# Hybrid decoder trunk on one core: another order of hooks and projection steps in the retention layer

## The chip, the core and the metric

The kernel runs on one core of one Trainium2 chip. TensorE multiplies matrices, VectorE (DVE), ScalarE (ACT) and GpSimd (POOL) work on elements, and SyncE (SP) issues DMAs. The metric is the device time of one execution in microseconds, lower is better.

## The reference

The trunk has two layers on 512 tokens of width 1024, in float32. The first mixes tokens by a gated MLP, the second by retention with 4 heads (key width 256, value width 512, chunks of 128); each is followed by a dense MLP of width 4096 with squared ReLU. The change lies in the second layer's mixer:

```python
def retention(xn, w_in, head_norm_g, w_out):
    proj = xn @ w_in                                   # (512, 1024) @ (1024, 6144)
    q, k, v, g = jnp.split(proj, [H * dk, 2 * H * dk, 2 * H * dk + H * dv], axis=-1)
    q, k = rotary(q, cos, sin), rotary(k * dk ** -0.5, cos, sin)
    ...
    # per chunk and head: o = (q k^T * decay) v + (q * decay) state ; state = state * decay + (k * decay)^T v
    ...
    o = rmsnorm(o, head_norm_g)
    o = o * jax.nn.silu(g)
    return o @ w_out

x = x + retention(rmsnorm(x, norm_mix_g[1]), ...)
x = x + squared_relu_mlp(rmsnorm(x, norm_ffn_g[1]), ...)
```

## The kernel before

**Precision.** Every float32 product is made of three TensorE passes over high and low parts (`mm3`, L290). Each weight tile `raw` is split into `wH` by a cast on ACT (L243) and `wL` by a subtraction on DVE (L250); both must be there before the matmuls of the tile.

**Fewer products.** The large projections (v, g and the output) are done as seven products of half blocks instead of eight (`seven`). Some products need sums of weight blocks: a base is loaded by SP (L173), and a second block is added to it in place by an accumulating DMA that GpSimd issues (L216). Some need sums of activations ("side sums": DVE L610 to L630, with a cast on ACT, L627). A product's result lands in a PSUM bank and is added by DVE into `vF` or `gF` (L512).

**Stages of the retention layer.** q and k are projected in `qk` steps of 24 matmuls (the script's `Q` and `q`, two for q and two for k of each head); v of heads 0 and 1 in steps `v`, of heads 2 and 3 in `w`; the gates g in `g` and `j`; the output in `o`. These have 12 matmuls each, only the last `o` has 24. The first `Q` has 48. The layer has no loop over chunks: all causal score blocks of a head are computed at once (`sc`, key chunk j against queries from j on), multiplied by the decay on DVE into `pm` and split (pH by ACT, pL by DVE), and multiplied with v (`av`, query chunk n, n+1 blocks of 3 matmuls). Then DVE multiplies with the gate into `gF` (L1194), ACT squares and sums (`sqh`, L1195), DVE and GpSimd form the norm's factor (`msh`, L1197; `rh`, L337) and ACT rescales `gF` (L1199). `yt` transposes a head's output on TensorE and ACT writes it to `ryF` (L1213).

**What sets the order.** The whole layer is one script, a string that `play` reads word by word. Each word runs the next step of the letter's stream: `v`, `g` and so on; after the step's matmuls are issued and the next weight tiles are prepared (three steps ahead), the actions in its brackets run, the hooks. Every engine takes its instructions in the order in which the program issues them, so the script fixes the order on all of them. `+G`, `+w` and `+j` make a stream's first weights known to the loader. I number steps by letter from 1: v11 is the eleventh `v`. The words of the hooks that matter here:

- `f3`: side sums 3 for the v projection; `k3`: store these sums to DRAM (L1056, SP); `F3`: fetch them back for the `w` projection into the tile `spx` (L1062, GpSimd), or form them anew for 0, 2 and 6. A step that needs a sum that isn't there calls for it itself.
- `R`: the token norm's factors; `p0`, `p1`: from here the rope (L1127 to L1137, DVE and ACT) of head 0's q and k may run.
- `sc01`: scores of head 0, key chunk 1; `av013`: outputs of head 0 for query chunks 1 and 3; `yt0013`: transposes of head 0, columns 0, 1, 3. `vs01`: the value split of chunk 1 (L1110 ACT, L1111 DVE); `si01`: silu of the gate (L1118).
- `T`: put the residual tokens away to DRAM; `t0`: bring half of them back (L1233). `y0`: fetch head 0's transposed output (L1222).
- `o10`: side sum 1 of the output projection, half 0. `X` and `x`: lend a further buffer (`more`) to the weight loads, and take it back.

`sc`, `av` and the first two `yt` of a head share two small PSUM banks.

Of the kernel before, what the change touches and what calls it, by code (L numbers as in the profile page):

```python
# [18 lines left out]
T = 512  # L19
# [69 lines left out]
def trunk(ctx, tc, x, norm_mix_g, norm_ffn_g, a_w_in, a_b_in, a_v_norm_g, a_w_s, a_b_s, a_w_out,  # L89
# [729 lines left out]
    def play(script, act, early, **streams):  # L819

        left = {k: list(v) for k, v in streams.items()}
        for word in script.split():
            if word[0] == "+":
                r = early[word[1]]
                assert r[0] not in raws
                raws.extend(r)
                continue
            name, _, rest = word.partition("(")
            todo = [act(w) for w in rest.rstrip(")").split(",") if w]
            hook = (lambda todo=todo: [(advance(), f()) for f in todo]) if todo else None  # L830
            if name == "-":
                do(hook)
            else:
                left[name].pop(0)(hook)
        assert not any(left.values()), left
# [418 lines left out]
    def act(word):  # L1254
# [22 lines left out]
    qs = [r for h in range(H) for r in qk_steps(h)]  # L1277
    do(begin_values)
    play("""
        Q(w0,f1) v v(R) v(k1) v(p0) v v(f3) q q(f5,f4) v v(k5) v(p1) v v v v +G v(T,sc00) g g g g(sc03,k4) g(vs0320) g  # L1280
        q(sc01) g g(k3) q(si00) g(sc02) g(F1) q g(si021,av00) g(vs01) q g q(si03,si110,sc10,av023) g(F4,av01,sc13) +w
        w(F3,sc12,yt02,si132,sc11) q(vs10123,yt0013,X) q(av101) w(x,av123) q(yt11) w(yt1320,sc20) w(sc21) w(sc22) w w
        w q(sc23) w(F5) w +j w w w j(X) w j q j j j j j j(vs2120) q(si210,t0,av20) j(vs23) j q j(si232,av221) j(y0)
        j(y1,o00,si31,av23) j(sc30,sc32,sc31,t1,o01,vs30) o(yt21,sc33) o o(vs3123,si302,o50,yt20)
        o(av301,o51,si33,av32,yt223) o(av33) o(o10) o(yt30123) o o o o(o20,o31) o o o o(o30) o o(o40,o21,o11) o o(o41)
        o o o(o60) o o o(o61) o o
    """, act, {"G": tG[:1], "w": tV[1:], "j": tG[1:], "o": tO}, v=prodV[0], g=prodG[0], w=prodV[1], j=prodG[1], o=prodO,
        Q=qs[:1], q=qs[1:])
    may["extra"] = True
# [143 lines left out]
```

## Time and profile before

| | |
|---|---|
| runs | 1633.93, 1333.93, 1336.11 us; median 1336.11 |
| the profiled execution | 1335.48 us, its span 1333.8 |
| mean granted TensorE clock | 0.993 |
| busy: PE, DVE, ACT, POOL | 98%, 65%, 53%, 11% of the span |
| retention layer | about 605 to 993 us of the span |

The profile is of one execution. Times within it count from the span's start. A row of the timeline gives start, length, engine, source line, operation, the tiles written and read, and in brackets how long the engine was idle before and what ended that. Matmul rows overlap their neighbours: the pace is the distance between starts.

### The profile page before, as it was taken

What the parts mean: (1) busy time and instruction counts of PE and PEld (TensorE: products, weight loads), DVE (VectorE), ACT (ScalarE), POOL (GpSimd) and SP (SyncE); (2) the same over time, 40 slices, a digit from 0 to 9 for tenths busy, and PEclk for the clock granted to TensorE, in tenths of its full rate; (3) what the DMA queues carried; (4) which work ended last, traced back from release to release, by engine and by line L of the source; (5) the groups of instructions that cost most, each with busy time, mean ns of one, the idle gap of its engine ahead of it and who ended that gap; (6) DMA issues with size and microseconds to landing.
All of it is one profiled execution on the core that took longest, in us unless ns stands there. A gap on an engine that the chain in (4) does not pass through costs nothing.

```text
span 1333.8 us, 15231 instructions
## 1 busy us (share of the span) xinstructions
PE 1307.0 (98%) x5914; PEld 1083.9 (81%) x5914; DVE 863.4 (65%) x1089; ACT 701.0 (53%) x1033; POOL 149.5 (11%) x130
## 2 busy tenths in 40 slices
PE   9999999999999999999999998998999999999997
PEld 7888887888888888888787886886888888888885
DVE  5654489844656655888855664566973565655697
ACT  5555544654445444655544662556754445444554
POOL 1000242000100001001100120012100000100003
PEclk9999999999999999999999999998999999999999
DMA  9765468751765759685997486779746475676763
GB/s 323 190 166 183 86 187 221 192 157 65 160 187 152 196 158 207 167 211 161 270 255 243 134 254 197 168 244 249 170 115 189 96 195 175 149 207 157 191 173 95
DMA packets 143065, 243.25 MB, mean 182 GB/s; under 512 B 4161, under 2 KB 56977, under 8 KB 140945
## 3 DMA queue, kind: packets, MB, share of 16 engines
q1 hardware_dynamic: 106192, 166.24, 36.4%
q0 software_dynamic: 36480, 75.50, 31.4%
q8 instruction: 46, 0.75, 0.2%
q10 hardware_dynamic: 320, 0.53, 0.1%
q14 instruction: 27, 0.21, 0.0%
HBM read 231.78 MB, written 10.49 MB: 182 GB/s over the span
## 4 chain that ended last, share of the span: by engine, by line
PE 88%; DVE 5%; DMA 2%; ACT 2%; issue 2%; POOL 1%; ACTq 0%; POOLq 0%; DVEq 0%
PE up L290 24%; PE u L290 6%; PE qk L290 5%; PE smwa L290 3%; DVE wL L250 2%; PE v L878 2%; PE smwc L290 2%; PE smroa L290 2%; PE smyoa L290 2%; PE v L290 2%; PE sm12a L290 2%; PE sm11a L290 2%; PE sm10a L290 2%; PE sm02a L290 2%; PE sm01a L290 2%
## 5 line engine op out<-in xcount | busy, mean ns | idle before, releaser
L250 DVE TENSOR_TENSOR wL<-raw,wH 128x1024 fp32r<-128x1024 f32 x263 | 326.5, 1250 | 157.9 <-issue 58.3
L243 ACT CAST wH<-raw 128x1024 fp32r<-128x1024 f32 x263 | 272.8, 1046 | 116.7 <-DMA raw<-in_b_w_in_dram 27.9
L290 PE MATMUL up<-hH,wH 128*128 128x512 f32 x480 | 186.7, 389 | 0.0
L290 PE MATMUL up<-hL,wH 128*128 128x512 f32 x480 | 186.7, 389 | 0.0
L290 PE MATMUL up<-hH,wL 128*128 128x512 f32 x480 | 186.7, 389 | 0.0
L978 ACT ACTIVATE aF<-up 128x512 f32<-128x512 f32 x60 | 36.0, 599 | 219.1 <-PE up L290 219.1
L250 DVE TENSOR_TENSOR wL<-more,wH 128x1024 fp32r<-128x1024 f32 x64 | 79.0, 1236 | 60.1 <-issue 34.1
L290 PEld LDWEIGHTS up<-hL,wH 128*128 128x128 f32 x480 | 90.1, 188 | 18.8
L290 PEld LDWEIGHTS up<-hH,wH 128*128 128x128 f32 x480 | 90.1, 188 | 18.7
L290 PEld LDWEIGHTS up<-hH,wL 128*128 128x128 f32 x480 | 90.1, 188 | 18.6
L216 POOL DMA_DIRECT2D raw<-in_mlp_w_dram x27 | 35.8, 1406 | 507.2 <-DMA raw<-in_mlp_w_dram 209.2
L243 ACT CAST wH<-more 128x1024 fp32r<-128x1024 f32 x64 | 66.9, 1047 | 30.3 <-PE sm11a L290 3.4
L630 DVE TENSOR_TENSOR sp<-aF,sp 128x512 fp32r<-128x512 f32 x48 | 31.0, 687 | 52.1 <-ACT sp L627 52.1
L290 PE MATMUL u<-hH,wH 128*128 128x512 f32 x128 | 50.2, 392 | 0.0
L290 PE MATMUL u<-hL,wH 128*128 128x512 f32 x128 | 49.8, 389 | 0.0
L290 PE MATMUL u<-hH,wL 128*128 128x512 f32 x128 | 49.8, 389 | 0.0
L290 PE MATMUL qk<-hH,wH 128*128 128x512 f32 x112 | 44.5, 397 | 1.3 <-DVE gF L512 1.3
L290 PE MATMUL qk<-hH,wL 128*128 128x512 f32 x112 | 44.3, 396 | 0.9 <-DVE wL L250 0.9
L290 PE MATMUL qk<-hL,wH 128*128 128x512 f32 x112 | 44.2, 395 | 0.0
L979 ACT ACTIVATE aF<-aF 128x512 f32<-128x512 f32 x64 | 40.5, 633 | 2.0
L742 ACT ACTIVATE gu<-uz,gT 128x512 f32<-128x512 f32 x16 | 11.6, 724 | 51.3 <-DVE uz L741 51.3
L216 POOL DMA_DIRECT2D raw<-in_b_w_in_dram x16 | 21.2, 1361 | 146.8 <-DVE wL L250 72.1
(512 smaller groups left out, 2943.7 us busy)
## 6 DMA issues: line engine op xcount, KB each, us to landing
raw<-in_mlp_w_dram SPq DMA_DIRECT2D x48, 1024.0 KB, 5.6
raw<-in_mlp_w_dram POOLq DMA_DIRECT2D x27, 1024.0 KB, 8.3
raw<-in_b_w_in_dram SPq DMA_DIRECT2D x26, 1024.0 KB, 7.3
more<-in_mlp_w_dram SPq DMA_DIRECT2D x24, 1024.0 KB, 5.3
raw<-in_b_w_in_dram POOLq DMA_DIRECT2D x16, 1024.0 KB, 9.7
raw<-in_a_w_in_dram SPq DMA_DIRECT2D x8, 1024.0 KB, 5.9
raw<-in_b_w_out_dram POOLq DMA_DIRECT2D x8, 1024.0 KB, 9.4
morew<-in_a_w_in_dram SPq DMA_DIRECT2D x7, 1024.0 KB, 7.9
```

The source lines that it names most:

```text
L216: nc.gpsimd.dma_start(out=r.tile, in_=src, accum_op=ALU.add)
L243: nc.scalar.copy(out=p.hi, in_=p.src)
L250: nc.vector.tensor_sub(out=p.lo, in0=p.src, in1=f32(p.hi))
L290: nc.tensor.matmul(ps, lhsT=a, rhs=b, start=start and i == 0, stop=stop and i == 2, skip_group_check=resumed)
L630: nc.vector.tensor_sub(out=lo, in0=vs[c], in1=f32(hi))
L742: nc.scalar.activation(gu[j][:, c, :], z, AF.Gelu_apprx_tanh, bias=gT[:, BU + f : BU + f + 1])
L878: nc.tensor.matmul(accs0[n], lhsT=h[kk][:, n * P : (n + 1) * P], rhs=w, start=kk == 0 and j == 0, stop=kk == 7 and j == 2)
L978: nc.scalar.activation(a, ps, AF.Relu)
L979: nc.scalar.activation(a, a, AF.Square)
```

## The change

Only the script of the retention layer is rewritten. No instruction is added or taken away: TensorE has 5250 rows of order and VectorE 989 in either kernel. What moves is the step at whose hook an action stands, the place of some `q` and `j` steps among the others, and with these the order of weight loads and accumulations.

```diff
@@ -1277,13 +1277,13 @@
     qs = [r for h in range(H) for r in qk_steps(h)]
     do(begin_values)
     play("""
-        Q(w0,f1) v v(R) v(k1) v(p0) v v(f3) q q(f5,f4) v v(k5) v(p1) v v v v +G v(T,sc00) g g g g(sc03,k4) g(vs0320) g
-        q(sc01) g g(k3) q(si00) g(sc02) g(F1) q g(si021,av00) g(vs01) q g q(si03,si110,sc10,av023) g(F4,av01,sc13) +w
-        w(F3,sc12,yt02,si132,sc11) q(vs10123,yt0013,X) q(av101) w(x,av123) q(yt11) w(yt1320,sc20) w(sc21) w(sc22) w w
-        w q(sc23) w(F5) w +j w w w j(X) w j q j j j j j j(vs2120) q(si210,t0,av20) j(vs23) j q j(si232,av221) j(y0)
-        j(y1,o00,si31,av23) j(sc30,sc32,sc31,t1,o01,vs30) o(yt21,sc33) o o(vs3123,si302,o50,yt20)
-        o(av301,o51,si33,av32,yt223) o(av33) o(o10) o(yt30123) o o o o(o20,o31) o o o o(o30) o o(o40,o21,o11) o o(o41)
-        o o o(o60) o o o(o61) o o
+        Q(w0,f1,k1) v(R) v v v(p0) v v q(f3) q(f5,f4) v v(p1) v v v(k5) v v(sc00) v +G g(T) g g g(sc03) g(k4,vs0320)
+        g(sc01) q g g(sc02) q(si01) g(k3,si00) g(vs01,F1) q q(av00) g(si03) g(av013,si02) g(av02) g(si110,sc10)
+        q(vs10123,sc11,F4) +w w(sc13,sc12,si132,F3) q(yt0013,X,yt02) q(av10123) w q w(yt10) w(yt12) w(x,yt113,sc20)
+        w(F5) q(X,sc21,sc23) w w w w(sc22) +j w w j w j w q j j j j j j j(vs20) q j(y0,vs23,si20,vs212,av20) q(si2132)
+        j(av212) j j(y1,o00,si31,t0,av23) j(sc30,sc33,sc32,sc31,t1,vs30) o(vs3123) o(si302,o50,yt20) o(yt21)
+        o(av32,o51,yt223,si33,av301) o(av33,o10) o o(yt30123) o o(o20,o01) o o(o31) o o o(o30) o(o60) o(o21)
+        o(o40,o11) o o(o41) o o o o(o61) o o o o
     """, act, {"G": tG[:1], "w": tV[1:], "j": tG[1:], "o": tO}, v=prodV[0], g=prodG[0], w=prodV[1], j=prodG[1], o=prodO,
         Q=qs[:1], q=qs[1:])
     may["extra"] = True
```

In the old script's terms: `k1`, `f3`, `k5`, `T`, `k4` and `k3` move by one to three steps, `p1` from v9 to v8; q6 stands ahead of g11 and g12 and carries `av00`; `av` of head 0 is spread over q6, g12 and g13, that of head 1 put together in the hook of q9; `F5` moves from w9 to w6 and q11 from behind w8 to behind w6; j1 and j2 stand ahead of w13 and w14; `t0` moves from q13 to j13; head 3's score block 3 moves from o1 to j14, and in o4 `av32` stands ahead of `av30` and `av31`; `o10`, `o20`, `o30`, `o60` and `o61` move to earlier o steps.

Three places show this in the engines' order. The first is VectorE around the rope of head 0's k, at v8 to v11 (`qkL_4632` and `qkL_4634` are its low parts, `smvc` a bank of the v projection). Before:

```order
L250 TENSOR_TENSOR wL_4867<-raw_4713,wH_4866 128x1024
L250 TENSOR_TENSOR wL_4883<-raw_4765,wH_4882 128x1024
L1127 TENSOR_TENSOR m_4908<-qk_4778,wide 128x512
L1128 TENSOR_TENSOR m_4911<-qk_4778,wide 128x512
L1129 TENSOR_TENSOR m_4909<-qk_4807,wide 128x512
L1130 TENSOR_TENSOR m_4910<-qk_4807,wide 128x512
L1131 TENSOR_TENSOR m_4908<-m_4908,m_4909 128x512
L1132 TENSOR_TENSOR m_4910<-m_4910,m_4911 128x512
L1137 TENSOR_TENSOR qkL_4632<-m_4908,qkH_4631 128x512
L1137 TENSOR_TENSOR qkL_4632<-m_4910,qkH_4631 128x512
L250 TENSOR_TENSOR wL_4905<-raw_4765,wH_4904 128x1024
L512 TENSOR_TENSOR vF_4775<-vF_4775,smvc_4727 128x512
```

and now:

```order
L250 TENSOR_TENSOR wL_4867<-raw_4713,wH_4866 128x1024
L1127 TENSOR_TENSOR m_4888<-qk_4771,wide 128x512
L1128 TENSOR_TENSOR m_4891<-qk_4771,wide 128x512
L1129 TENSOR_TENSOR m_4889<-qk_4807,wide 128x512
L1130 TENSOR_TENSOR m_4890<-qk_4807,wide 128x512
L1131 TENSOR_TENSOR m_4888<-m_4888,m_4889 128x512
L1132 TENSOR_TENSOR m_4890<-m_4890,m_4891 128x512
L1137 TENSOR_TENSOR qkL_4634<-m_4888,qkH_4633 128x512
L1137 TENSOR_TENSOR qkL_4634<-m_4890,qkH_4633 128x512
L250 TENSOR_TENSOR wL_4883<-raw_4765,wH_4882 128x1024
L250 TENSOR_TENSOR wL_4917<-raw_4765,wH_4916 128x1024
L512 TENSOR_TENSOR vF_4768<-vF_4768,smvc_4727 128x512
```

Of the two weight splits ahead of the rope's eight instructions, the second (`wL_4883`) is now behind them.

The second place is GpSimd from q5 to w9: `raw` tiles are accumulations of weights, `spx` are the fetched sums (the first of each list are sums 1, the last sums 5), `rh` the norm factors of one query chunk each. Before:

```order
L1062 DMA spx_5334<-sums_4694 128x2048
L216 DMA raw_5369<-in_b_w_in_dram 128x4x512
L337 TENSOR_TENSOR rh<-msh,mhalf 128x1 x3
L1062 DMA spx_5581<-sums_5113 128x2048
L337 TENSOR_TENSOR rh<-msh,mhalf 128x1
L1062 DMA spx_5627<-sums_5236 128x2048
L216 DMA raw_5369<-in_b_w_in_dram 128x4x512
L337 TENSOR_TENSOR rh<-msh,mhalf 128x1 x4
L216 DMA raw_5877<-in_b_w_in_dram 128x4x512
L216 DMA raw_5880<-in_b_w_in_dram 128x4x512
L216 DMA raw_5369<-in_b_w_in_dram 128x4x512
L1062 DMA spx_6108<-sums_4888 128x2048
```

and now:

```order
L216 DMA raw_5337<-in_b_w_in_dram 128x4x512
L1062 DMA spx_5342<-sums_4631 128x2048
L337 TENSOR_TENSOR rh<-msh,mhalf 128x1 x4
L1062 DMA spx_5617<-sums_5133 128x2048
L1062 DMA spx_5663<-sums_5316 128x2048
L216 DMA raw_5337<-in_b_w_in_dram 128x4x512
L337 TENSOR_TENSOR rh<-msh,mhalf 128x1 x4
L216 DMA raw_5877<-in_b_w_in_dram 128x4x512
L216 DMA raw_5880<-in_b_w_in_dram 128x4x512
L1062 DMA spx_6007<-sums_4956 128x2048
L216 DMA raw_5337<-in_b_w_in_dram 128x4x512
```

The accumulation that stood behind the first fetch stands ahead of it, no fetch stands between head 0's four `rh`, and the fetch of sums 5 stands ahead of the third accumulation into the same tile (`raw_5369` before, `raw_5337` now), behind the two that precede it.

The third place is ScalarE at o4 and o5, around the outputs of head 3 (`av_6877` before and `av_6845` now are its query chunk 2). Before:

```order
L1213 ACTIVATE ryF_6754<-yt_6821,gT 128x512
L243 CAST wH_6839<-raw_6679 128x1024
L1195 ACTIVATE sqh_6850,ssh<-av_6845 128x512
L1199 ACTIVATE gF_6378<-gF_6378,rh 128x512
L1195 ACTIVATE sqh_6863,ssh<-av_6855 128x512
L1199 ACTIVATE gF_6378<-gF_6378,rh 128x512
L627 CAST spro_6868<-saro_6869 128x512 x2
L1118 ACTIVATE gF_6378<-gF_6378,r_80 128x512
L1195 ACTIVATE sqh_6888,ssh<-av_6877 128x512
```

and now:

```order
L1213 ACTIVATE ryF_6798<-yt_6821,gT 128x512
L243 CAST wH_6839<-more_6042 128x1024
L1195 ACTIVATE sqh_6856,ssh<-av_6845 128x512
L1199 ACTIVATE gF_6378<-gF_6378,rh 128x512
L627 CAST spro_6861<-saro_6862 128x512 x2
L1213 ACTIVATE ryF_6798<-yt_6869,gT 128x512
L1213 ACTIVATE ryF_6798<-yt_6875,gT 128x512
L1118 ACTIVATE gF_6378<-gF_6378,r_80 128x512
L1195 ACTIVATE sqh_6887,ssh<-av_6882 128x512
```

The first square behind the cast was that of query chunk 0, and is that of chunk 2 now; the chunks 0 and 1 follow behind the two transposes of head 2. The cast ahead reads `raw_6679` before, and the lent tile `more_6042` now.

## The prediction

> **What bounds the kernel now.** I read the page's busy times first, then the windows over the retention layer (605 to 993 us of the span), then the waits of TensorE there, and then the rows around each wait.
>
> ```profile
> span 1333.8 us, 15231 instructions
> PE 1307.0 (98%) x5914; PEld 1083.9 (81%) x5914; DVE 863.4 (65%) x1089; ACT 701.0 (53%) x1033; POOL 149.5 (11%) x130
> 605.00:992.00 387.00, 372.47 (x1675) 307.42 (x1673) 264.39 (x358) 212.74 (x321) 49.86 (x45) 0.98 0.78 211
> 720.00:740.00 20.00, 17.80 (x71) 13.96 (x70) 11.26 (x15) 8.19 (x11) 1.88 (x2) 0.91 0.56 140
> 800.00:820.00 20.00, 15.00 (x63) 12.29 (x62) 6.68 (x8) 4.40 (x5) 0.00 (x0) 0.91 0.81 224
> 890.00:935.00 45.00, 39.28 (x176) 31.59 (x175) 29.36 (x46) 28.63 (x50) 8.82 (x8) 0.92 0.85 223
> 935.00:1000.00 65.00, 64.64 (x307) 53.74 (x306) 56.39 (x72) 42.49 (x66) 5.16 (x4) 1.00 0.61 144
> ```
>
> The columns of a window are its length, then the busy time and count of PE, PEld, DVE, ACT and POOL, the granted clock, the DMA share and GB/s. The kernel is bound by TensorE: 1307.0 of 1333.8 us. In the retention layer PE is idle 387.00 - 372.47 = 14.5 us, and three windows hold nearly all of it (2.2 + 5.0 + 5.7), with the clock at 0.91 or 0.92 in the same three. That bounds the change: no matmul is added or removed, so it can save the stalls and slow stretches and no more, some 20 us, while 2% of this kernel is 26.7 us.
>
> ```profile
> PE smwa L290 <- DMA spx<-sums: 5.0, 1, 5.0
> PE av L290 <- ACT sqh L1195: 4.0, 1, 4.0
> ```
>
> These are the two longest of PE's waits there (the columns: total, times, longest). Each occurs once, as do the shorter ones, so the change is priced place by place, in program order. What a wait costs beyond itself is seen at the stall in the first of the three windows:
>
> ```profile
> 728.68 0.39 PE L290 MATMUL smga<-wH,hL 128*128 128x512 f32 x1
> 730.33 0.47 PE L290 MATMUL qk<-hH,wH 128*128 128x512 f32 x1 [1.26 <-DVE gF L512]
> 730.64 0.39 PE L290 MATMUL qk<-hL,wH 128*128 128x512 f32 x1
> 731.97 0.61 PE L290 MATMUL qk<-hH,wL 128*128 128x512 f32 x1 [0.94 <-DVE wL L250]
> 735.36 0.52 PE L290 MATMUL qk<-hL,wH 128*128 128x512 f32 x1
> 735.72 0.40 PE L290 MATMUL qk<-hH,wL 128*128 128x512 f32 x1
> ```
>
> Matmuls start 0.23 us apart at the full clock, but from 731.97 to 735.36 eight steps take 3.39 us, 0.42 each: about 1.6 us lost after the waits have ended. The whole stall: 730.33 - 728.68 - 0.23 = 1.4, 731.97 - 730.64 - 0.23 = 1.1, and the 1.6, in sum 4.1. I call the last part the gate's price, 1.7 with its edges.
>
> **Place 1, v10 to v13 (k, f3, p1 moved).** `p1` now comes one v step earlier, so the rope of head 0's k stands ahead of a weight split on DVE which stood ahead of it.
>
> ```profile
> 647.84 3.49 DVE L250 TENSOR_TENSOR wL<-raw,wH 128x1024 fp32r<-128x1024 f32 x3
> 651.24 0.68 DVE L1127 TENSOR_TENSOR m<-qk,wide 128x512 f32<-128x512 f32 x1
> 655.00 1.29 DVE L1137 TENSOR_TENSOR qkL<-m,qkH 128x512 fp32r<-128x512 f32 x2
> 656.21 1.22 DVE L250 TENSOR_TENSOR wL<-raw,wH 128x1024 fp32r<-128x1024 f32 x1
> 655.01 0.39 PE L290 MATMUL smva<-wL,spv 128*128 128x512 f32 x1
> 661.64 0.47 PE L290 MATMUL smva<-wH,hH 128*128 128x512 f32 x1 [1.25 <-DVE vF L512]
> ```
>
> The rope is 656.21 - 651.24 = 5.0 us. The third of the three splits ended at 651.3 and was needed at 655.01 (slack 3.7); behind the rope it ends at 656.3. The hook of f3, one step later, also puts one split ahead of the side sums, which may delay DVE by none or all of 1.22; I take 0.75, so 657.1: a new wait of 2.1. The wait at 661.64 then shrinks, since PE comes 2.1 later and DVE 0.75 later to the same add. Net later by 2.1 - 1.25 + what is left of the old wait, about 0.15: **+1.0**. Bounds: 0 (slack covers it) to +2.7 (the gate's price on top).
>
> **Place 2, q5 to g14.** What held PE at 730.33 was a queue on GpSimd:
>
> ```profile
> 724.60 1.28 POOL L216 DMA_DIRECT2D raw<-in_b_w_in_dram  x1 [17.12 <-issue]
> 725.39 1.09 POOL L337 TENSOR_TENSOR rh<-msh,mhalf 128x1 f32<-128x1 f32 x1
> 726.52 0.72 ACT L1199 ACTIVATE gF<-gF,rh 128x512 f32<-128x512 f32 x1 [6.88 <-POOL rh L337]
> 729.51 1.28 DVE L512 TENSOR_TENSOR gF<-gF,smgb 128x512 f32<-128x512 f32 x2
> ```
>
> The accumulation of a weight tile was late (the profile shows nothing that it waited for; I take it to be its base, whose load comes through SP's queue). Behind it stood the power rh of av00, behind that on ACT the rescale of L1199 (6.88 us idle) with two weight casts, and behind those DVE's add of gF and the split at 730.70. After the change q6 is drawn ahead of g11 and g12 and av00 hangs on it, while the weight tile's load is due earlier; in GpSimd's order the accumulation and the first fetch stand ahead of all four rh. av00's scores come some 5 us of matmuls later against the accumulation. I expect rh at its natural time and no wait here: **-4.1**. Bounds: 0 if the base again arrives last, -4.1 if it doesn't. The four av of head 0 then fall at separate steps. The cover of the weight splits is DVE's free time, 20.00 - 11.26 = 8.7 us in that window; if that were gone the wait would reappear at q7 as a wL wait of about 1.
>
> **Place 3, q7 to w2.** The four av of head 1 now run in one hook, through two small banks. A bank comes free when sqh has read it:
>
> ```profile
> 718.95 0.60 ACT L1195 ACTIVATE sqh<-av 128x512 f32<-128x512 f32 x1 [2.02 <-DVE gF L1194]
> 718.23 0.69 DVE L1194 TENSOR_TENSOR gF<-av,gF 128x512 f32<-128x512 f32 x1 [2.10 <-PE av L290]
> ```
>
> DVE's 0.69 and ACT's 0.60 follow each other: 718.23 to 719.55, 1.3 us. av11's six matmuls cover 6 x 0.23 = 1.4 of av12's wait, so with nothing ahead it is nil; with one cast of 1.04 ahead on ACT (the row at 916.45 below) it is up to 1.0 for each of two. I take half: **+1.0**, bounds 0 to +3.7 (two waits and the gate). yt, vs and silu only change hooks; ACT is 8.19 of 20.00 busy here and hides them, at most 0.7 each if not.
>
> **Place 4, the fetch of sums 5.** This was the largest wait:
>
> ```profile
> 788.29 1.28 POOL L216 DMA_DIRECT2D raw<-in_b_w_in_dram  x1 [1.49 <-PE sc L290]
> 798.12 1.27 POOL L216 DMA_DIRECT2D raw<-in_b_w_in_dram  x1 [8.54 <-DVE wL L250]
> 798.87 1.11 POOL L1062 DMA_DIRECT2D spx<-sums  x1
> raw<-in_b_w_in_dram POOLq DMA_DIRECT2D x1, 1024.0 KB, 16.4
> spx<-sums POOLq DMA_DIRECT2D x4, 1024.0 KB, 7.9
> 814.36 0.77 PE L290 MATMUL smwa<-wH,spx 128*128 128x512 f32 x1 [5.00 <-DMA spx<-sums]
> ```
>
> The two DMA rows are the accumulation of 788.29 and the median of the layer's four fetches. The fetch of 798.87 stood behind an accumulation that waited 8.54 us for its buffer, and PE took it at 814.36, 15.5 us later. In the new order it stands ahead of that accumulation, behind the one of 788.29; its own buffer comes free with head 1's last transposes, about 790. With 7.9 it lands at 798, with 15.5 at 805.5; but two accumulations are under way, the second until 788.3 + 16.4 = 804.7, and the fetch shares their queue: I estimate 805 to 808, near the loaded rows, and take 807.2. PE came to w9 at 814.36 - 5.00 - 0.2 = 809.2 before; without place 2 and with places 1 and 3 it comes at 809.2 - 4.1 + 2.0 = 807.1, less the scores sc22 moved behind it (0.7), about 806.3. Wait about 1.0. A lone wait of 1.25 at 661.64 was followed by matmuls at the full pace, so I charge no gate. Before: 5.0 + 0.3 at the edges + 1.7 = 7.0. **-6.0**, bounds -7.0 (no wait) and +2.1: if the fetch lands no earlier than it did, w9 begins where it did, and what places 1 to 3 gain, 4.1 - 2.0, is given back.
>
> **Place 5, head 3's scores and outputs.**
>
> ```profile
> 916.45 1.04 ACT L243 CAST wH<-raw 128x1024 fp32r<-128x1024 f32 x1 [3.99 <-DMA raw<-in_b_w_out_dram]
> 917.40 0.59 ACT L1195 ACTIVATE sqh<-av 128x512 f32<-128x512 f32 x1
> 918.14 0.79 PE L290 MATMUL av<-vvH,pH 128*128 128x512 f32 x1 [3.97 <-ACT sqh L1195]
> 922.14 1.63 PE L1211 MATMUL yt<-ident,gF 128*128 128x128 f32 x8
> 923.53 0.48 PE L290 MATMUL smrod<-wH,spro 128*128 128x512 f32 x1
> ```
>
> ACT holds a cast for a weight tile that lands at 916.4, and the sqh that frees PE's bank is queued behind it; the landing ends the stall. In the new order the cast still stands ahead of the first sqh, but av32 (nine matmuls) and the eight transposes run before the stall and only av31's six are left after it. Before, 923.53 - 918.14 = 5.4 remained; after, 6 x 0.43 = 2.6: -2.8. Of that, av33 waits for sqh of av30 (0.7) and the transposes of head 3 for one L1199 (0.72): -1.4. The fourth score block, now in j14's hook, makes the later two wait for DVE's multiplication into pm, by my estimate 0.8 and 2.2, with up to two splits of 1.22 ahead of it; they fall ahead of the same landing and are swallowed. **-1.4**, bounds -4 (they cost nothing, full clock) and +2.5 (they aren't swallowed and pay the gate).
>
> **Place 6, the o steps.** Side sums o10, o20, o30, o60 and o61 come one to seven steps earlier; words for sums that the next step would call itself do nothing. DVE is 56.39 of 65.00 busy in that window, PE 64.64: they are hidden so far, **0**. One pair of side sums is 2.57 us on DVE, from these rows:
>
> ```profile
> 909.93 1.28 DVE L616 TENSOR_TENSOR saro<-ryG 128x512 f32<-128x512 f32 x2
> 911.36 1.29 DVE L630 TENSOR_TENSOR spro<-saro,spro 128x512 fp32r<-128x512 f32 x2
> ```
>
> Bounds: none, to the second rival. The stores k and T, the tile X, tokr's load on SP and the base loads of the MLP behind it that take other buffers cost nothing: 820 to 890 and the MLP show no wait of PE.
>
> Sum: +1.0 - 4.1 + 1.0 - 6.0 - 1.4 = -9.5, from the profiled execution's 1335.5 (span 1333.8 and 1.7 around it), 0.6 below the median of the three times: **1326.0**.
>
> **The rule of the Trainium skill that I weighed.** The Trainium skill, "TensorE: Matmul & The Clock Gate", section "HAM oscillation — how this bites in real kernels", says that what must be avoided are idle gaps of over some 3.4 us. By that rule no new wait (at most 2.2) would pay. The rows at 730.33 to 735.36 disagree: two waits of 1.26 and 0.94 were followed by the slow 3.4 us. By the rule the sum would be about 1 us lower, by the rows the third rival's.
>
> **The rivals.**
> 1. *All three stalls go* (fetch near 7.9 us, new waits nil, the landing of place 5 earlier by its accumulation's shorter queue): -4.1 - 7.0 - 6 = -17: 1318. For it: 7.9 is the median fetch. Against it: two accumulations ahead, and place 5 ends by a landing. 0.15.
> 2. *Slower: VectorE becomes the bound in the o steps.* DVE has 8.6 us free in 65; three pairs of side sums that come early put 3 x 2.57 = 7.7 us ahead of splits that PE waits for, and two such waits close together pay 1.7 each: +11.1, so 1337. It decides for slower once the added waits in the o steps exceed 9.5. For it: 87% busy. Against it: the total is the same and most moves are of one step. 0.13.
> 3. *The gate at the new waits.* Places 1, 3 and 4 each pay 1.7: -9.5 + 5.1 = -4.4: 1331. For it: the rows of place 2; against it: 661.64. 0.15.
> 4. *It does little:* the moves only shift waits, since two of the three stalls end with a landing. The fetch lands at 812, 2.3 before it did, which swallows places 1 to 3, and place 5's landing is as late as it was: -2.3, so 1333, up to 1336. For it: three transfers share the queue around 790. Against it: the order takes an 8.54 us wait from ahead of the fetch. 0.17.
>
> **How the numbers follow.** The forecast, 1321 to 1331, has 0.40; the rivals 0.15, 0.13, 0.15 and 0.17. The low end goes to 1318, leaving out half of the first; the high end to 1338, leaving out the second's tail and place 1's and 5's upper bounds together. Only 26.7 us, about what a measurement can tell from no change, would be faster by over 2%, more than all stalls; slower by that needs five new stalls. So 0.01, 0.98, 0.01.
>
> **What would show it.** Right: clock 1.00 and no wait over 0.5 in q5 to q7; a wL wait near v11 of about 2; spx issued near 790 and landing before 808; six, not nine, av matmuls after the wH cast of place 5. Wrong: rh again behind an accumulation; spx landing after 812; a clock under 1.00 near v11 or q9; waits for wL between 935 and 990.

## The result and the profile after

The changed kernel takes 1326.03 us (median of four, 1325.73 to 1327.03), against 1336.11 before (median of three, 1333.93 to 1337.71). A fourth run of the kernel before was slow, at 1633.93 us, and is left out. The ratio is 0.9927, 95% interval 0.9908 to 0.9947: it is faster by 0.7%, clear of noise and well within 2%. The forecast was 1326.0. The total was met, but three of its terms came out otherwise and their errors cancelled; the experiments say which.

The page's head, a window over the layer (it ends 7 us earlier than the one of before) and TensorE's waits, of the changed kernel:

```profile
span 1324.4 us, 15227 instructions
PE 1304.6 (99%) x5914; PEld 1081.8 (82%) x5914; DVE 863.3 (65%) x1089; ACT 701.9 (53%) x1033; POOL 149.6 (11%) x130
```

```profile
605.00:985.00 380.00, 372.29 (x1686) 307.62 (x1685) 265.69 (x361) 214.05 (x322) 50.12 (x45) 0.99 0.79 215
```

```profile
PE smwa L290 <- ACT vF L508: 3.2, 1, 3.2
PE av L290 <- ACT sqh L1195: 1.6, 3, 1.0
PE sc L290 <- DVE pm L1173: 1.5, 2, 1.3
PE smrod L290 <- DVE wL L250: 0.8, 1, 0.8
PE smva L290 <- DVE wL L250: 0.6, 1, 0.6
```

TensorE is idle for 7.7 us of this window instead of 14.5. (The window holds 11 matmul rows more than the one of before, so the two busy times are not of the same work.) The waits have other names: none is for a fetch any more, none for `gF` at q7; the longest is for ACT writing a tile of v.

A wait is not all that is lost, since slow matmuls follow some of them. So I also add up, from the rows of the matmuls, by how much each starts later after the one before than at the full pace (0.227 us for 128x512; 0.172, 0.118 and 0.068 for narrower ones; only excesses over some 0.03 count, and with that limit at 0.04 a sum changes by up to 0.3). The stages are cut at the first matmul of g, at the first of w, at 779 us (about w4), at the first of j, and at the MLP's first; j and the o steps are one column, since nothing is lost in the j steps ahead of the scores of head 3. Layer is the time from its first matmul to the MLP's first.

| profile of | v | g, q5 to q7 | head 1's av | 779 to j | j and o | layer |
|---|---|---|---|---|---|---|
| before | 1.74 | 4.81 | 0.72 | 7.63 | 12.75 | 391.91 |
| changed | 1.17 | 0.27 | 1.59 | 5.77 | 9.45 | 382.81 |
| difference | -0.6 | -4.5 | +0.9 | -1.9 | -3.3 | -9.1 |
| forecast | +1.0 | -4.1 | +1.0 | -6.0 | -1.4 | -9.5 |

**Place 2** is as forecast. GpSimd of the changed kernel:

```profile
719.24 1.28 POOL L216 DMA_DIRECT2D raw<-in_b_w_in_dram  x1 [26.71 <-PE qk L290]
724.99 1.48 POOL L337 TENSOR_TENSOR rh<-msh,mhalf 128x1 f32<-128x1 f32 x1 [3.87 <-DVE msh L1197]
```

The accumulation is issued at 719.2 instead of 724.6, and `rh` runs 5.7 us behind it, waiting for nothing but its own input.

**Place 4** is not. SP's store of head 1's turned output, GpSimd's fetch, ACT's first write into the tile of v, and TensorE at w7 (first the rows of the timeline, then each DMA's time to landing):

```profile
787.75 0.57 POOL L1062 DMA_DIRECT2D spx<-sums  x1 [2.37 <-PE yt L1211]
788.34 0.34 SPq L1216 DMA_DIRECT2D ys<-ryF  x1
801.22 1.09 ACT L508 ACTIVATE vF<-smwa 128x512 f32<-128x512 f32 x2 [10.06 <-DMA ys<-ryF]
801.87 0.50 PE L290 MATMUL smwa<-wH,spx 128*128 128x512 f32 x1 [3.21 <-ACT vF L508]
803.74 0.63 PE L290 MATMUL smwa<-wL,spx 128*128 128x512 f32 x1
807.23 0.39 PE L290 MATMUL smwa<-wL,spx 128*128 128x512 f32 x1
```

```profile
spx<-sums POOLq DMA_DIRECT2D x1, 1024.0 KB, 15.6
ys<-ryF SPq DMA_DIRECT2D x1, 1024.0 KB, 12.8
```

The fetch was issued as forecast (787.75 for "about 790") and landed at 803.4, 3.8 us before the 807.2 that I took and before w9 came to it at 809.1; the step that I expected to wait 1.0 waits for nothing. But w7, two steps earlier, stood for 3.2 us: its bank had to be emptied by ACT into `vF`, and ACT waited 10.1 us for the store, which was still reading the buffer that `vF` was to have. Then the slow clock came, to 807.2: 5.1 us in all.

**Place 5**, ACT and TensorE of the changed kernel:

```profile
891.93 0.52 PE L290 MATMUL sc<-qkH 128*128 128x384 f32 x1 [1.31 <-DVE pm L1173]
892.25 0.52 PE L290 MATMUL sc<-qkL,qkH 128*128 128x384 f32 x1
895.81 0.63 PE L290 MATMUL smroa<-wH,spro 128*128 128x512 f32 x2
909.03 1.05 ACT L243 CAST wH<-more 128x1024 fp32r<-128x1024 f32 x1 [2.18 <-DMA more<-in_b_w_out_dram]
910.72 0.50 PE L290 MATMUL av<-vvH,pH 128*128 128x512 f32 x1 [0.37 <-ACT sqh L1195]
```

The cast for the landing tile still stands ahead of the square on ACT, but TensorE hardly waits for it: 0.37 instead of 3.97, and no slow clock follows. The score blocks at j14 wait 0.16 and 1.31 (forecast 0.8 and 2.2) and are followed by 3.6 us of slow matmuls.

### The profile page after: what moved, and what is told of

Read it like the earlier page. It is cut to its first block, busy times and chain, and to the rows that moved or that the text cites. A ratio compares the mean times of both kernels' runs of the same rounds, so it can differ in the third digit from the quotient of the medians.

```text
span 1324.4 us, 15227 instructions
## 1 busy us (share of the span) xinstructions
PE 1304.6 (99%) x5914; PEld 1081.8 (82%) x5914; DVE 863.3 (65%) x1089; ACT 701.9 (53%) x1033; POOL 149.6 (11%) x130
## 4 chain that ended last, share of the span: by engine, by line
PE 82%; issue 8%; DVE 4%; DMA 3%; ACT 2%; POOL 1%; ACTq 0%; POOLq 0%; DVEq 0%
PE up L290 24%; PE u L290 6%; PE qk L290 5%; PE smwa L290 3%; PE v L878 2%; PE smroc L290 2%; PE smwc L290 2%; PE smga L290 2%; PE smroa L290 2%; PE smyoa L290 2%; PE v L290 2%; PE sm12a L290 2%; PE sm11a L290 2%; PE sm10a L290 2%; PE sm01a L290 2%
## 5 line engine op out<-in xcount | busy, mean ns | idle before, releaser
L250 DVE TENSOR_TENSOR wL<-raw,wH 128x1024 fp32r<-128x1024 f32 x267 | 330.0, 1245 | 160.5 <-issue 62.0
L243 ACT CAST wH<-raw 128x1024 fp32r<-128x1024 f32 x267 | 277.7, 1047 | 110.2 <-DMA raw<-in_b_w_in_dram 24.1
L250 DVE TENSOR_TENSOR wL<-more,wH 128x1024 fp32r<-128x1024 f32 x60 | 75.7, 1262 | 65.2 <-PE up L290 29.7
L243 ACT CAST wH<-more 128x1024 fp32r<-128x1024 f32 x60 | 62.6, 1047 | 27.7 <-PE sm01a L290 3.4
L630 DVE TENSOR_TENSOR sp<-aF,sp 128x512 fp32r<-128x512 f32 x48 | 31.0, 688 | 52.1 <-ACT sp L627 52.1
```

The source lines that it names most:

```text
L243: nc.scalar.copy(out=p.hi, in_=p.src)
L250: nc.vector.tensor_sub(out=p.lo, in0=p.src, in1=f32(p.hi))
L630: nc.vector.tensor_sub(out=lo, in0=vs[c], in1=f32(hi))
```

## The experiments

All start from the changed kernel; the diffs show words of its script. The kernel before took 1335.9 to 1338.0 beside them. Each row is one profiled execution, and its time is that of one execution, but for the last two, which are medians of four. As the layer's first matmul starts anywhere from 605.0 to 607.7 from run to run, the stage sums are the sharper measure.

| profile of | v | g, q5 to q7 | head 1's av | 779 to j | j and o | layer | time |
|---|---|---|---|---|---|---|---|
| transposes earlier | 2.42 | 0.27 | 1.54 | 4.62 | 8.90 | 382.21 | 1326.04 |
| fetch back at w9 | 2.68 | 0.27 | 1.57 | 9.03 | 9.27 | 387.25 | 1331.31 |
| q11 back behind w8 | 1.35 | 0.27 | 1.56 | 13.54 | 9.28 | 390.52 | 1334.42 |
| score block back at o1 | 2.20 | 0.27 | 1.58 | 6.84 | 8.85 | 384.20 | 1328.66 |
| q6 and av00 back | 1.21 | 5.43 | 1.72 | 4.50 | 9.14 | 386.34 | 1330.38 |
| q6 back alone | 2.56 | 0.27 | 2.38 | 5.52 | 9.30 | 384.52 | 1328.91 |
| av00 earlier alone | 2.36 | 0.28 | 1.43 | 5.26 | 9.26 | 383.02 | 1328.76 |
| av32 last | 2.41 | 0.27 | 1.58 | 5.51 | 9.36 | 383.66 | 1327.37 |
| score block and av back | 0.99 | 0.28 | 1.56 | 5.01 | 8.66 | 380.93 | 1324.38 |
| two loads of SP back | 1.13 | 0.27 | 1.56 | 4.77 | 9.36 | 381.49 | 1325.26 |
| two edits together | 1.14 | 0.27 | 1.56 | 5.59 | 8.78 | 381.94 | 1325.5 |
| changed, again | 1.05 | 0.28 | 1.56 | 6.73 | 8.95 | 382.95 | 1326.29 |

Two groups show in the column v, with the same code up to there. The wait at v11 is for a weight split that stands behind the rope on VectorE. Ahead of both, VectorE stands for a cast on ACT (1.65 us in the changed kernel, 3.0 with the transposes earlier), and the cast for an accumulating DMA that GpSimd issues 21.2 us after the layer's first matmul. The cast before the change, in the changed kernel and with the transposes earlier:

```profile
636.28 1.05 ACT L243 CAST wH<-raw 128x1024 fp32r<-128x1024 f32 x1 [4.98 <-DMA raw<-in_b_w_in_dram]
634.70 1.06 ACT L243 CAST wH<-raw 128x1024 fp32r<-128x1024 f32 x1 [3.62 <-DMA raw<-in_b_w_in_dram]
636.57 1.05 ACT L243 CAST wH<-raw 128x1024 fp32r<-128x1024 f32 x1 [4.98 <-DMA raw<-in_b_w_in_dram]
```

From the layer's first matmul (605.20, 604.97 and 605.49) these are 31.1, 29.7 and 31.1 us. The accumulation took 9.8 us before the change, 8.3 to 8.7 in the seven profiles that lose 1.0 to 1.4, and 9.6 to 10.0 in the six that lose 2.2 to 2.7. So the profile of before compares with the six, not with the changed kernel's.

### Place 4: the fetch goes back

```diff
-w(F5) q(X,sc21,sc23) w w w w(sc22)
+w q(X,sc21,sc23) w w w(F5) w(sc22)
```

> Compared with the changed kernel, the fetch of sums 5 goes back to w9 and everything else stays. Theory 'store', slowed by the fetch beside it: the store of head 1 takes 8.6 us again instead of 12.8 and w7 doesn't wait, but the fetch is issued behind the third accumulation, about 795, lands near 810, and w9, due at 804, waits 6 us and then runs slowly: 1328 to 1330. Rival 'the fetch doesn't slow the store': w7 waits 3.2 us as before and w9 waits about 3 more: 1329 to 1331, with two waits in the profile. If the early fetch brought nothing at all: 1326.

1331.31 us; the stretch from 779 to j loses 9.0. ACT, GpSimd and TensorE of this kernel, and the store and the fetch:

```profile
793.38 1.11 ACT L508 ACTIVATE vF<-smwa 128x512 f32<-128x512 f32 x2
803.12 0.57 POOL L1062 DMA_DIRECT2D spx<-sums  x1 [6.03 <-DMA ys<-ryF]
811.96 0.77 PE L290 MATMUL smwa<-wH,spx 128*128 128x512 f32 x1 [5.43 <-DMA spx<-sums]
```

```profile
ys<-ryF SPq DMA_DIRECT2D x1, 1024.0 KB, 12.2
spx<-sums POOLq DMA_DIRECT2D x1, 1024.0 KB, 8.7
```

w7's missing wait is as the first theory said. The time lies 1.3 us above its range, and the v steps, ahead of the edit, lose 1.5 us more than in the changed kernel. But the theory's reason falls: without the fetch beside it the store took 12.2 us, no better than 12.8. What changed is who waits for it. Now the tile of v is written at once and the fetch stands 6.03 us for the store. One of the two gets the buffer that head 1's output leaves, whichever is used second; my prediction gave each of them a free one. With the fetch early it is v.

### Place 4: q11 goes back

```diff
-w(F5) q(X,sc21,sc23) w w w w(sc22)
+w(F5) w w q(X,sc21,sc23) w w(sc22)
```

> Compared with the changed kernel, q11 goes back from behind w6 to behind w8 with its hooks; the fetch stays early. Theory 'store': w7 comes 6.9 us earlier while the store lands at about 801 as it did, so w7 waits 10 us instead of 3.2, the layer ends 0 to 1 us later, since the same landing ends the wait but 6.9 us of work stand behind it: 1331 to 1334. Rival 'fetch': w7 and w8 run through, q11 covers the fetch, and the time is 1323 to 1326.

1334.42, 0.4 above the range of "store" and 8 us off for "fetch". GpSimd and TensorE at w7, and the store:

```profile
794.19 1.11 POOL L1062 DMA_DIRECT2D spx<-sums  x1
802.02 0.79 PE L290 MATMUL smwa<-wH,spx 128*128 128x512 f32 x1 [9.63 <-ACT vF L508]
```

```profile
ys<-ryF SPq DMA_DIRECT2D x1, 1024.0 KB, 12.1
```

w7 starts at 802.0, as with q11 ahead of it (801.9); the 6.9 us of q11 and its scores are then still to do. The fetch did not stay early in time: without q11 ahead of w7 and w8, a weight accumulation is issued ahead of it, and it goes out at 794.2, 6.4 us later than in the changed kernel. The tile of v has the late buffer all the same, as the fetch still comes first in the program's order. F5's move without q11's makes this stretch worse than it was before the change, 13.5 us lost against 7.6: q11 covers most of the store.

### Place 4: the transposes come earlier

```diff
-w(yt10) w(yt12) w(x,yt113,sc20)
+w(yt102) w(yt113) w(x,sc20)
```

> Compared with the changed kernel, head 1's four transposes come one w step earlier (columns 0 and 2 after w3, 1 and 3 after w4 instead of 0, 2, and 1 with 3 after w3, w4 and w5), so the store of its turned output is issued about 2.7 us earlier. Theory 'store': the 3.2 us wait of w7 ends when this store has read the buffer that v's next tile takes; then the wait falls to 0.5 or less, no slow clock follows, place 4 loses about 1 us instead of 5.1, and the time is about 1322. Rival 'fetch': the wait is really for the fetch of sums 5 or for DMA bandwidth as such; the store lands at about 801 again and the time stays at 1326.

A miss for the expected size. ACT, TensorE and the store:

```profile
802.57 1.08 ACT L508 ACTIVATE vF<-smwa 128x512 f32<-128x512 f32 x2 [9.64 <-DMA ys<-ryF]
803.22 0.50 PE L290 MATMUL smwa<-wH,spx 128*128 128x512 f32 x1 [2.78 <-ACT vF L508]
```

```profile
ys<-ryF SPq DMA_DIRECT2D x1, 1024.0 KB, 15.1
```

Issued earlier, the store took 15.1 us, so it lands at nearly the same time and the wait is 2.8 instead of 3.2; no slow clock follows it here. The rows point to the transfer that holds the store up, a weight load that SP issues. The load and the store before the change, and the load in the changed kernel:

```profile
788.38 0.34 SPq L1216 DMA_DIRECT2D ys<-ryF  x1
791.09 0.37 SPq L173 DMA_DIRECT2D raw<-in_b_w_in_dram  x1
783.64 0.37 SPq L173 DMA_DIRECT2D raw<-in_b_w_in_dram  x1
```

Before, the load is issued 2.7 us behind the store, which takes 8.6 us. In all thirteen profiles of the new order the load is issued ahead of it, by 4.7 us or, with the transposes earlier, by 1.9, and the store lands 3.9 to 4.0 us after the load, whenever it was issued. No run moves this load alone, so that it is the cause is not shown. The dependency on the store is shown; a cure is not.

### Place 2: three ways back

```diff
-q q(av00) g(si03) g(av013,si02) g(av02)
+q g(av00) g(si03) q(av013,si02) g(av02)
```

> Compared with the changed kernel, q6 goes back behind g12 and av00 back to g11; all other moves stay. If place 2 was read rightly, the weight base is loaded some 4 us later again, its accumulation on GpSimd comes at about 724, ahead of av00's rh, which is wanted at about 720, and the stall at q7 returns: the g steps lose 3 to 5 us instead of 0.3, time 1329 to 1331. Rival 'another cause' (the silu and value splits that changed hooks): no stall, 1326.

GpSimd, ACT and TensorE of this kernel:

```profile
725.59 1.28 POOL L216 DMA_DIRECT2D raw<-in_b_w_in_dram  x1 [15.01 <-DMA raw<-in_b_w_in_dram]
726.38 1.09 POOL L337 TENSOR_TENSOR rh<-msh,mhalf 128x1 f32<-128x1 f32 x1
727.50 0.72 ACT L1199 ACTIVATE gF<-gF,rh 128x512 f32<-128x512 f32 x1 [7.52 <-POOL rh L337]
736.77 0.50 PE L290 MATMUL av<-vvH,pH 128*128 128x512 f32 x1 [3.28 <-ACT sqh L1195]
```

The stall is back, 5.4 us in the g steps, and by the same queue: ACT waits 7.52 for `rh`, which stands behind an accumulation whose base landed late. The profile now names the base, which the row of before had left open. TensorE meets it at another instruction, av03 instead of q7.

Then each of the two moves alone (`av00` on g12 is one g step, 2.7 us of matmuls, behind g11, and not 5.4, as the first expectation has it):

```diff
# q6 back alone
-q q(av00) g(si03) g(av013,si02) g(av02)
+q g(si03) g(av00) q(av013,si02) g(av02)
# av00 earlier alone
-q q(av00) g(si03)
+q(av00) q g(si03)
```

> Compared with the changed kernel, q6 goes back behind g12, but av00 keeps its distance (it hangs on g12, 5.4 us of matmuls later than g11). Theory 'later outputs': av00's rh is wanted at about 725, as the late accumulation comes at about 724, so nothing waits and the time is 1326 to 1327. Rival 'earlier base': the stall goes only because the base is loaded earlier, which this undoes; 3 us or more come back, 1329 or above.

> Compared with the changed kernel, av00 hangs on q5, 5.4 us of matmuls earlier, and q6 stays ahead of g11. Theory 'earlier base': the accumulation comes at 719, before rh is wanted at about 720, so nothing waits: 1326. Rival 'later outputs': what counted was av00's place, rh stands behind the accumulation and 2 to 4 us come back: 1328 to 1330.

1328.91 and 1328.76. The times lie 2.9 and 2.7 above the changed kernel's median, but not in the g steps, which lose 0.27 and 0.28: av00's layer starts 2.7 us later and is as long as the changed one; in q6's the v steps, ahead of any edit, lose 1.4 more, and the scores among head 1's steps lose 1.0. GpSimd and ACT, first with q6 back, then with av00 earlier:

```profile
727.33 1.28 POOL L216 DMA_DIRECT2D raw<-in_b_w_in_dram  x1 [15.04 <-DMA raw<-in_b_w_in_dram]
729.24 0.73 ACT L1199 ACTIVATE gF<-gF,rh 128x512 f32<-128x512 f32 x1 [4.82 <-POOL rh L337]
```

```profile
723.02 1.28 POOL L216 DMA_DIRECT2D raw<-in_b_w_in_dram  x1 [26.79 <-issue]
725.53 0.73 ACT L1199 ACTIVATE gF<-gF,rh 128x512 f32<-128x512 f32 x1 [5.41 <-POOL rh L337]
```

ACT still waits 4.8 or 5.4 us for `rh`, and TensorE never hears of it. Either move is enough; 7 us on ACT reach TensorE there and 5 do not. "Earlier base" falls by the first of the two runs and "later outputs" by the second, each having claimed the whole gain.

### Place 5: three ways back

```diff
# score block back at o1
-j(sc30,sc33,sc32,sc31,t1,vs30) o(vs3123)
+j(sc30,sc32,sc31,t1,vs30) o(sc33,vs3123)
# av32 last
-o(av32,o51,yt223,si33,av301)
+o(av301,o51,yt223,si33,av32)
```

> Compared with the changed kernel, head 3's score block 3 goes back from j14's hook to o1's. Theory 'bank': the block in the middle made the next two wait for DVE (0.2 and 1.3 us) and these brought the slow clock, 3.8 us in all; now 1.8 as before the change, and the time is about 1324. Rival 'landing': what is won there is given back at the av blocks, whose wait ends with the cast of a landing weight tile; that wait grows by 2 and the time stays at 1326.

> Compared with the changed kernel, head 3's av30 and av31 go back ahead of av32. If place 5 was read rightly, the wait for the square behind the cast of the landing weight tile leaves nine matmuls and the eight transposes behind it instead of six matmuls: PE leaves this group 1.5 us later without and 3 us later with the slow clock: 1327.5 to 1329. Rival 'the landing decides alone': the end of the group doesn't move, 1326.

The score block's return saves 3.1 of the 3.8 us at j14 and loses 2.5 at the next steps, where two waits for weight splits of VectorE appear (2.4 with their edges); j and o lose 8.85. Its 1328.66 lies above what either theory said, and the rest of it comes from ahead of the edit: the v steps lose 1.0 more and the stretch from 779 to j 1.1. The order of the outputs makes no difference: 9.36 (its 1327.37 has 1.2 more in the v steps). So I undid both, with the transposes where they were:

```diff
-j(sc30,sc33,sc32,sc31,t1,vs30) o(vs3123)
+j(sc30,sc32,sc31,t1,vs30) o(sc33,vs3123)
-o(av32,o51,yt223,si33,av301)
+o(av301,o51,si33,av32,yt223)
```

> Compared with the changed kernel, both head 3's score block 3 (to o1) and the order of its outputs (30, 31, 32, then head 2's transposes) go back to what they were. Theory 'either is enough': each alone cost nothing, but without both, PE reaches the group early and has nine matmuls and the transposes left when the tile lands: the o steps lose 11 to 12.5 us instead of 9, time 1328 to 1330. Rival: the gain of 3 us in the o steps comes from an earlier landing alone; the o steps lose 9 to 10, time 1326 to 1327.

8.66, and 1324.38: "either is enough" falls. The first matmul of head 3's scores in this kernel, to time by, then the load of the landing tile's base, its accumulation and ACT's cast; and load and accumulation before:

```profile
886.29 0.39 PE L290 MATMUL sc<-qkH 128*128 128x512 f32 x1
887.34 0.38 SPq L173 DMA_DIRECT2D more<-in_b_w_out_dram  x1
892.92 1.31 POOL L216 DMA_DIRECT2D more<-in_b_w_out_dram  x1 [5.25 <-ACT pH L1174]
907.19 1.05 ACT L243 CAST wH<-more 128x1024 fp32r<-128x1024 f32 x1 [1.39 <-DMA more<-in_b_w_out_dram]
```

```profile
895.53 1.48 SPq L173 DMA_DIRECT2D raw<-in_b_w_out_dram  x3
901.33 1.30 POOL L216 DMA_DIRECT2D raw<-in_b_w_out_dram  x1 [5.47 <-ACT pH L1174]
```

The cast comes 20.9 us after the scores' start, and 22.95 before the change (916.45, scores at 893.50): the landing itself is earlier against TensorE. Half of that is the load of the base, which goes out 1.05 us after the scores' start instead of 2.0; most of the rest is the accumulation, 14.3 us instead of 15.1. TensorE's wait there is shorter (1.4 us instead of 4.0) and no slow matmuls follow it, which cost 2.8 us before. I tried one cause of the earlier landing, two loads on SP's queue:

```diff
-j(vs20) q j(y0,vs23,si20,vs212,av20) q(si2132) j(av212) j j(y1,o00,si31,t0,av23)
+j(vs20) q(t0) j(vs23,si20,vs212,av20) q(si2132) j(av212) j(y0) j(y1,o00,si31,av23)
```

> Compared with the changed kernel, the fetch of head 0's turned output goes back to j12 and the load of the residual tokens to q13, ahead of it in SP's queue. Theory 'landing': the side sums of the output projection then come later on DVE, the split that frees the next weight tile too, and the tile of o5 lands 1 to 2 us later against PE; the o steps lose 11 us or more instead of 9, time 1328 or above. Rival: the landing isn't moved by these two, o steps 9, time 1326.

1325.26, 9.36 lost: not these two. What lets the base's load go out earlier stays open. Not undone are the lent buffer's move from j1 to q11 (the tile is a lent one now) and the side sums of the o steps, nor, elsewhere, the moves of `p1`, `f3`, the stores and j1 and j2.

### Two edits together, and the changed kernel again

`both` has the earlier transposes and the score block at o1.

> The changed kernel with two things taken from the single trials: head 1's transposes one w step earlier, and head 3's score block 3 back at o1. The stages add up if they are independent: 1.1 us less lost in the w steps and 0.4 in the o steps, so 1324 to 1325, against 1326 for the changed kernel in the same runs. Rival: what varies from execution to execution (the wait at v11, the slow clock at j14) is as large, and both have the same time.

> The changed kernel itself, beside the others on one chip: 1326, 0.993 of the kernel before; a second profile shows which of its waits repeat. The wait of w7 (3.2 us) and of the score block at j14 (1.3) should; the slow clock behind the latter may not.

1325.50 (1323.64 to 1325.97; ratio 0.9917, 0.9895 to 0.9938) and 1326.29 (0.9927, 0.9909 to 0.9944). The intervals overlap: no version beyond the changed one is shown to be faster. In `both` the store, issued at 785.8, took 15.3 us, and w7 still waits 3.0. The second profile of the changed kernel repeats the wait of w7 and the waits at j14, and here the slow clock behind them too.

## Why the prediction came out

- **Bound.** No more than some 20 us could be saved; 9.1 were.
- **Place 1**, +1.0 forecast. Against the six profiles whose accumulation took as long as before, the v steps lose +0.5 to +0.9: there the split ends 51.6 to 52.1 us after the layer's first matmul, as forecast (657.1 - 605.2 = 51.9), and the term was right. In the seven others, the changed kernel's own two among them, the accumulation was some 1.3 us shorter, the split ends at 50.4 to 50.8, and the difference is -0.4 to -0.8. As kernels with the same code there fall into both groups, the change alone doesn't decide this; why the accumulation takes 8.4 or 9.8 us stays open. The new wait at v11 is in all thirteen, and the old one at 661.64 is gone.
- **Place 2**, -4.1: measured -4.5, by the queue that was named. That two moves did it together was wrong: either does.
- **Place 3**, +1.0: measured +0.9, in small gaps; the longest of its waits for `sqh` is 0.2, where two of a half were forecast, so the size is right for another reason.
- **Place 4**, -6.0: measured -1.9, in the second profile -0.9. The failed step is "its own buffer comes free with head 1's last transposes", taken as free of cost to others, and that w7 and w8 run through: the early fetch passes the late buffer, and the store's landing, on to the tile of v. That landing is also later than before (12.8 us after the store's issue instead of 8.6); the prediction had no term for it. The gate that I didn't charge came too (1.9).
- **Place 5 and 6**, -1.4 and 0: measured -3.3, here -3.8 in the second profile. The step that failed is that the landing "ends the stall" as it did: it came earlier against TensorE, by 1.3 us in the changed kernel and by 2.05 with both moves undone. The order of av32, the transposes and av31, on which the -1.4 stood, is worth nothing. What the score block's place costs at j14 is mostly swallowed, as I said, but by waits for weight splits in the next steps and not by the landing.
- **Rivals.** The o steps didn't become bound by VectorE (one wait of 0.8 for `wL`). Of the three places that were to pay the gate only place 4 did; j14 paid it too, in three of ten profiles.

So 1326 was in part luck: in the sum of the profiled execution, 4 us of missing gain at place 4 were made up by 2 at place 5 and 1.6 at place 1, and the last goes with one accumulation that was shorter, for a reason that is open.

## What to carry to other kernels

When a transfer is moved ahead, ask which buffer it takes and who would have had it: the wait may pass to another engine's write two steps earlier, with a new name in the profile. A forecast by places should be judged by places; a total that fits proves no step. Before a difference in one stage is credited to the change, see whether other kernels with the same code there show it. To credit one of two moves, undo each alone and then both.

## What the runs showed of the hardware

The slow clock doesn't follow a wait of given length. The wait of 1.31 at j14 above was followed by slow matmuls to 895.6; the same wait with the transposes earlier was not:

```profile
892.36 0.45 PE L290 MATMUL sc<-qkH 128*128 128x384 f32 x1 [1.30 <-DVE pm L1173]
892.64 0.34 PE L290 MATMUL sc<-qkL,qkH 128*128 128x384 f32 x1
892.82 0.33 PE L290 MATMUL sc<-qkH,qkL 128*128 128x384 f32 x1
```

Of ten profiles with this order of score blocks, three lose some 3.8 us there and seven 2.2, with the same two waits: 1.6 us that the waits don't explain. Both profiles of the changed kernel are among the three, so it isn't shown that this varies between executions of one kernel. The Trainium skill, "TensorE: Matmul & The Clock Gate", "Part 1: The HAM clock gate", describes a free-running window of activity, which would fit a clock that depends on where a gap falls; no run here shows that window. The limit of some 3.4 us for idle gaps, quoted in the prediction from the Trainium skill, does not fit these rows.
